# Two-layer hybrid trunk on one core: constants packed into two transfers, modulation weights in rotating slots, a lead of six staggered weight blocks

## The chip, the cores and the metric

The program runs on one core of one Trainium2 chip. A core has a matrix engine (TensorE, PE in the profile), a vector engine (VectorE, DVE), an activation engine (ScalarE, ACT), a general engine (GpSimd, POOL) and an engine that here only issues transfers (SyncE, SP). Every engine runs its own instructions in a fixed order and waits on semaphores for the others. The metric is the device time of one execution in microseconds (us), the lower the better.

## The reference

Two layers act on 256 context tokens and 256 latent tokens of 1024 features. Every sub-layer is RMSNorm, a shift and scale that a linear map makes from the conditioning vector, a body, and a gated residual add. The bodies are a SwiGLU with 2816 hidden features (half weight, twice per layer) and a mixer: in layer 0 eight attention heads beside 512 channels of an S5 state-space model, in layer 1 Hyena convolutions beside RG-LRU recurrences. Cut to what matters here:

```python
def adaln_params(cond, w, b):
    m = jax.nn.silu(cond) @ w + b
    return m.reshape(cond.shape[0], 1, N_MOD, D_MODEL)

def ffn_half_step(h, m, k, g, w_gate, w_up, w_down):
    shift, scale, gate = m[:, :, 3 * k], m[:, :, 3 * k + 1], m[:, :, 3 * k + 2]
    hn = modulate(rmsnorm(h, g), shift, scale)
    return h + 0.5 * gate * swiglu(hn, w_gate, w_up, w_down)
...
    for i in range(DEPTH):
        last = i == DEPTH - 1
        m_lat = adaln_params(c, mod_w[i], mod_b[i])
        m_ctx = adaln_params(c_ctx[None, :], mod_w[i], mod_b[i])
        ...
        lat = ffn_half_step(lat, m_lat, 0, norm_ffn1[i], *ffn1)
        cx = ffn_half_step(cx, m_ctx, 0, norm_ffn1[i], *ffn1)
        ...
            y_ctx, y_lat = even_mixer(h_ctx, h_lat, cos, sin, ...)
        lat = lat + m_lat[:, :, 5] * y_lat
        ...
    return rmsnorm(lat, final_norm)
```

## The kernel before

Features lie on the 128 partitions (eight feature tiles), the 512 tokens of both streams on the free axis. A float32 product is made as three matrix products of split parts (`mm3`, L145 to L151): high weight by high x (L149), high weight by low x (L150), low weight by high x (L151). `wload` (L136) loads a raw weight block of 128 x 1024 on SP's queue (L139), ACT casts its high part (L141), and DVE makes the low part (L142).

The Tile framework's scheduler sets the order of each engine's instructions from the order of the program, from priorities (`high_priority`) and from its own cost model; so an edit in one place can move instructions elsewhere. SP and ACT issues take eight completion semaphores in rotation, and an issue waits until the transfer that used its semaphore before has landed.

The work around the change is the lead, the first norm and the first products of the first half SwiGLU:

- `build` (L1233) loads the residual in four transfers (L1242), the condition `ct`, the S5 parameters (L463), the modulation weights of the first sub-layer `mw0` in eight tiles of two 512 KB halves (L1266), five constants behind tile 0 (L103: `sel`, `ident`, `modb`, `gain`, `sig`), and four weight blocks behind tiles 0 and 1. Eight smaller constants (`qkvn`, `rope`, `s5_d`, `s5_bg`, `lru_p`, `hy_cw`, `hy_b`, `lru_cw`) are loaded one by one where their stages begin in the program. Tile 5 of `mw0` sits in the `m` slots, tile 6 in the `sc` slot, the others in the `h` slots. The background modulation's condition `c2` (1 MB, L199) needs the `sc` slot too.
- `square_add` (L265, L269, L270) squares the residual on ACT and adds on DVE. `rstd_stats` sums over partitions on PE (L236) and finds 1/rms in three Newton steps on DVE (L241 to L249); `rstd_rows` spreads it over the partitions with the identity matrix (L256).
- `mod_first` (L172) makes shift and scale of one feature tile on PE: sixteen matmuls with `mw0` (L179), a copy on ACT (L188), four small matmuls with `sel` (L191), then bias and gain on DVE (`mod_fix`, L165, L168). Its PSUM tile comes from the pool `pm` (six buffers), which the products use too; the pool `ps` has two buffers.
- `norm_tile` (L278) gives a normalised tile: L287 on DVE, the high part on ACT (L292), the low part on DVE (L294). `norm_proj` (L297) with `lead` then makes, tile by tile, the products of the four blocks, twelve matmuls of 512 columns per tile.

Background work runs beside the SwiGLU: `mod_job` makes the later shifts, scales and gates on DVE (L215), and `s5_prepare` makes the S5 matrices (`s5_small` L455 first). In the even mixer, eight S5 passes (`s5_states`, `s5_out`) are interleaved with the products of the heads; a pass loads its matrices just ahead of its use (L920, L924) into the `x` slots. `lru_decay` (L1039) makes the constant `kap` of layer 1 from `lru_p`.

## Time and profile before

| what | us |
| --- | --- |
| median of three runs | 1826.03 |
| lowest and highest of them | 1825.6, 1826.72 |
| span of the profiled execution | 1825.2 |
| PE busy in the span | 1742.0 (95%) |
| DVE busy | 1307.9 (72%) |
| ACT busy | 684.6 (38%) |
| POOL busy | 37.0 (2%) |

The profile is one execution of the program. Its own time is given as its span, 1825.2 us, from the first to the last recorded work; the timed runs lie 0.4 to 1.5 us above it. Rows name an engine, a line of the kernel (L149), and the tiles written and read (out<-in). "Idle before" names what the engine waited for. PEclk is the clock that TensorE was granted, as a share of full speed.

### The profile page before, as it was taken

The page shows a single profiled execution, that of the slowest core. Times are in us where ns is not written, and L with a number is a line of the kernel's source. Part 1 is how long each engine was busy: PE and PEld are TensorE (multiplying, and loading weights), DVE is VectorE, ACT ScalarE, POOL GpSimd, SP SyncE. Part 2 cuts the span into 40 slices and gives each one's busy share as a digit, 9 for nine tenths or more (in the row PEclk, how much of TensorE's full clock was granted, in tenths as well). Part 3 has the DMA queues.
Part 4 walks back from the last instruction along what each step waited for, and adds up shares of the span by engine and source line. Part 5 has one row for each costly group of instructions (what it writes and reads, how often), then busy time and mean ns, then how long its engine had stood idle before and what let it go on. Part 6 is the DMA issues. An engine that isn't in the chain of part 4 may idle for free.

```text
span 1825.2 us, 24880 instructions
## 1 busy us (share of the span) xinstructions
PE 1742.0 (95%) x9364; PEld 1456.1 (80%) x9364; DVE 1307.9 (72%) x2582; ACT 684.6 (38%) x1082; POOL 37.0 (2%) x57
## 2 busy tenths in 40 slices
PE   5999999997999998999999999999999989789997
PEld 3778777787877787778888888888888888589997
DVE  7999999898578667775666677766653476975555
ACT  4433333333345654222222233222122247554442
POOL 0000000001000000000000010000000000010000
PEclk9999999998998999999999999999999999889998
DMA  8466666652465452664554533554533225236562
GB/s 320 167 213 203 207 205 202 211 193 96 124 187 160 131 170 89 191 208 141 159 184 150 161 116 124 175 174 152 171 116 93 81 81 198 71 130 194 181 190 92
DMA packets 108057, 292.64 MB, mean 160 GB/s; under 512 B 21217, under 2 KB 36449, under 8 KB 107681
## 3 DMA queue, kind: packets, MB, share of 16 engines
q1 hardware_dynamic: 102368, 287.39, 49.2%
q10 hardware_dynamic: 4928, 2.10, 0.6%
q0 software_dynamic: 640, 1.57, 0.3%
q8 instruction: 73, 1.20, 0.3%
q14 instruction: 48, 0.39, 0.1%
HBM read 272.20 MB, written 18.28 MB: 159 GB/s over the span
## 4 chain that ended last, share of the span: by engine, by line
PE 83%; DVE 9%; DMA 3%; ACT 2%; issue 1%; SPq 1%; DVEq 0%; ACTq 0%
PE mm L149 26%; PE mm L150 26%; PE mm L151 26%; DVE w L142 1%; DMA raw<-in_wgu_dram 1%; DVE acc L270 1%; DVE rs_y L249 1%; ACT w L141 1%; DMA x<-d_g 1%; DMA h<-in_modw_dram 1%; DMA x<-d_v 0%; SPq L943 0%; DVE rs_a L247 0%; DVE nt L287 0%; DVE junk L215 0%
## 5 line engine op out<-in xcount | busy, mean ns | idle before, releaser
L150 PE MATMUL mm<-x,w 128*128 128x512 f32 (+1 forms) x1792 | 631.6, 355 | 3.3 <-DVE x L294 3.3
L151 PE MATMUL mm<-x,w 128*128 128x512 f32 (+1 forms) x1792 | 630.1, 354 | 0.0
L149 PE MATMUL mm<-x,w 128*128 128x512 f32 (+1 forms) x1792 | 613.9, 357 | 11.4 <-ACT x L292 9.9
L141 ACT CAST w<-raw 128x1024 fp32r<-128x1024 f32 (+2 forms) x328 | 332.5, 1018 | 532.8 <-issue 267.4
L142 DVE TENSOR_TENSOR w<-raw,w 128x1024 fp32r<-128x1024 f32 (+2 forms) x318 | 376.5, 1187 | 164.0 <-ACT w L141 163.3
L149 PEld LDWEIGHTS mm<-x,w 128*128 128x128 f32 x1792 | 334.9, 192 | 65.8 <-ACT x L292 10.9
L150 PEld LDWEIGHTS mm<-x,w 128*128 128x128 f32 x1792 | 343.4, 192 | 52.2 <-DVE x L294 4.3
L151 PEld LDWEIGHTS mm<-x,w 128*128 128x128 f32 x1792 | 343.1, 192 | 49.3 <-issue 1.8
L215 DVE CUSTOM_DVE_ANT_0 junk<-m,sc 128x1024 f32<-128x1024 f32 x256 | 312.4, 1220 | 2.2
L149 PE MATMUL mm<-h,w 128*128 128x512 f32 (+1 forms) x776 | 270.3, 351 | 0.0
L150 PE MATMUL mm<-h,w 128*128 128x512 f32 (+1 forms) x776 | 270.1, 349 | 0.0
L151 PE MATMUL mm<-h,w 128*128 128x512 f32 (+1 forms) x776 | 269.8, 349 | 0.0
L150 PEld LDWEIGHTS mm<-h,w 128*128 128x128 f32 x776 | 146.2, 188 | 21.2 <-issue 1.4
L149 PEld LDWEIGHTS mm<-h,w 128*128 128x128 f32 x776 | 145.9, 189 | 21.5 <-issue 1.1
L151 PEld LDWEIGHTS mm<-h,w 128*128 128x128 f32 x776 | 146.2, 188 | 20.3 <-issue 0.4
L394 DVE SCALAR_TENSOR_TENSOR res<-mm,mraw,res 128x256 f32<-128x256 f32 x192 | 86.1, 479 | 97.1 <-PE mm L151 96.6
L422 DVE TENSOR_TENSOR h<-h,mm 128x512 f32<-128x512 f32 (+1 forms) x88 | 54.6, 620 | 125.2 <-PE mm L151 108.5
L421 ACT ACTIVATE h<-mm 128x512 f32<-128x512 f32 (+1 forms) x88 | 47.9, 544 | 238.3 <-PE mm L151 238.2
L292 ACT ACTIVATE x<-nt,mraw 128x256 fp32r<-128x256 f32 x88 | 43.0, 506 | 75.3 <-DVE nt L287 75.2
L156 DVE TENSOR_TENSOR h<-h,h 128x512 fp32r<-128x512 f32 (+1 forms) x88 | 54.4, 618 | 0.0
L155 ACT CAST h<-h 128x512 fp32r<-128x512 f32 (+1 forms) x88 | 49.6, 564 | 9.1 <-DVE h L422 9.0
L269 ACT ACTIVATE sq<-res 128x256 f32<-128x256 f32 x84 | 33.3, 413 | 50.4 <-DVE res L394 38.5
(324 smaller groups left out, 1437.1 us busy)
## 6 DMA issues: line engine op xcount, KB each, us to landing
raw<-in_wgu_dram SPq DMA_DIRECT2D x176, 512.0 KB, 3.6
m<-in_modw_dram SPq DMA_DIRECT2D x130, 512.0 KB, 4.2
raw<-in_wd_dram SPq DMA_DIRECT2D x64, 512.0 KB, 3.7
raw<-in_wd_dram SPq DMA_DIRECT2D x32, 384.0 KB, 3.3
raw<-in_od_in_dram SPq DMA_DIRECT2D x20, 512.0 KB, 3.5
h<-in_modw_dram SPq DMA_DIRECT2D x12, 512.0 KB, 10.4
raw<-in_ev_in_dram SPq DMA_DIRECT2D x10, 512.0 KB, 3.8
d_mb<-mbt SPq DMA_DIRECT2D x16, 256.0 KB, 3.0
```

Source lines behind the costliest of these rows:

```text
L141: nc.scalar.copy(w[:, 0, :n], raw[:, :n])
L142: (nc.gpsimd if pool else nc.vector).tensor_sub(w[:, 1, :n], raw[:, :n], w[:, 0, :n])
L149: mm(ps, lhsT=wh, rhs=xh, start=first and i == 0, stop=False)
L150: mm(ps, lhsT=wh, rhs=xl, start=False, stop=False)
L151: r = mm(ps, lhsT=wl, rhs=xh, start=False, stop=last and i == n - 1)
L155: self.nc.scalar.copy(hi, src)
L156: self.nc.vector.tensor_sub(lo, src, hi)
L215: nc.vector.tensor_tensor_reduce(self.junk, w, self.sc[:, v, :], 1.0, 0.0, ALU.mult, ALU.add, raw[:, dt, v : v + 1])
L292: self.last_act = nc.scalar.activation(x[:, 0, c0:c1], y, AF.Identity, bias=b)
L394: self.nc.vector.scalar_tensor_tensor(r, ps[:, c0:c1], gate[:, i, VEC[h] : VEC[h] + 1], r, op0=ALU.mult, op1=ALU.add)
L421: nc.scalar.activation(s[:, 0, lo:hi], pg[:, lo:hi], AF.Silu)
L422: nc.vector.tensor_mul(s[:, 1, lo:hi], s[:, 0, lo:hi], pu[:, lo:hi])
```

## The change

It does these things:

- Thirteen constants lie in one array `small` of 128 x 698 floats. `packed` loads its first 333 columns (`sel`, `ident`, `modb`, `gain`, `sig`; 170 KB) with one transfer on ACT's queue and the other 365 columns (187 KB; `rope` is padded from 64 to 128 partitions) with one transfer on POOL's queue, both ahead of all other work on these queues; `ct` moves to ACT's queue too. All later loads of single constants go.
- Every fourth `mw0` tile sits in the `m` slots, the others in the `h` slots in rotation. The `sc` slot stays free, so `c2` goes out on SP as soon as its turn comes: behind `mw0` tile 3, ahead of the lead blocks 4 and 5.
- `LEAD = (0, 0, 1, 2, 3, 4)`: six blocks instead of four are made in the lead. A block is loaded behind the `mw0` tile that its number names, and its products start with that feature tile, where it also makes up for the tiles before. Blocks 4 and 5 keep their two parts in `h` slots.
- `mod_first` takes its PSUM tile from `ps`, since six blocks fill `pm`.
- The first step of `s5_prepare` is emitted behind the loads and with a lower priority.

```diff
+SMALL = dict(sel=(2,), ident=(P,), modb=(2, 9, KT), gain=(7, KT), sig=(3,), qkvn=(5,), s5_d=(4,), s5_bg=(4,), lru_p=(2, 3, 4),
+             hy_cw=(12, 4), hy_b=(4,), lru_cw=(4, 5), rope=(NTOK,))
+LEAD = (0, 0, 1, 2, 3, 4)
...
+    def packed(self):
+        n = [math.prod(sh) for sh in SMALL.values()]
+        tl = self.const([P, sum(n)], "small")
...
+        cut = sum(n[:5])
+        self.nc.scalar.dma_start(tl[:, :cut], self.t["small"][:, :cut])
+        self.nc.gpsimd.dma_start(tl[:, cut:], self.t["small"][:, cut:])
...
+        if tag is None:
+            w = self.wp.tile([P, 2, 1024], F32R, tag="w", name=self.uid("w"))
+            hi, lo = w[:, 0], w[:, 1]
+        else:
+            hi, lo = (self.slot(tag, [P, 1024], F32R) for _ in range(2))
...
     def mod_first(self, i):
-        ps = self.pm()
+        ps = self.ps()
...
-                for w, ps in zip(ws, pss):
-                    self.mm3(ps, self.wparts(w, KT)[i : i + 1], self.parts(xs[i : i + 1], 0, T2), i == 0, i == KT - 1)
+                for w, ps, k0 in zip(ws, pss, LEAD):
+                    for j in range(0 if k0 == i else i, i + 1) if k0 <= i else ():
+                        self.mm3(ps, self.wparts(w, KT)[j : j + 1], self.parts(xs[j : j + 1], 0, T2), j == 0, j == KT - 1)
...
-        self.lp = self.const([P, 2, 3, 4], "lru_p", self.t["lru_p"])
+        self.lp = self.sml["lru_p"]
...
+        nc.scalar.dma_start(self.ct, t["ct"])
+        self.packed()
...
-            if i == 0:
-                nc.sync.dma_start(self.ct, t["ct"])
-                s5 = self.s5_prepare()
-                next(s5)
...
-            if i == 6:
-                w = self.slot("sc", [P, 2, 4, 2 * P])
-                self.mw0.append([w[:, r] for r in range(2)])
-            else:
-                self.mw0.append([self.slot("m" if i == 5 else "h", [P, 4, 2 * P]) for _ in range(2)])
+            self.mw0.append([self.slot("m" if i % 4 == 3 else "h", [P, 4, 2 * P]) for _ in range(2)])
             for r in range(2):
                 nc.sync.dma_start(self.mw0[i][r], t["modw0"][i, :, r])
-            if i == 0:
-                small()
-            if i < 2:
-                self.w0 += [self.wload(t["wgu"][0, i, g], D) for g in range(2)]
+            for b, k in enumerate(LEAD):
+                if k == i:
+                    self.w0.append(self.wload(t["wgu"][0, b // 2, b % 2], D, tag=None if b < 4 else "h"))
+        s5 = self.s5_prepare()
+        with self.tc.high_priority(offset=-400):
+            next(s5)
```

The scheduler then orders the engines anew. Three places matter here. The lines of the changed kernel are its own: its L296 is L269 of before, L206 is L179, L218 is L191, L263 is L236, L283 is L256, L176 is L149, L169 is L142, L314 is L287, L954 to L956 are L928 to L930.

First, ACT in the statistics (`sq` are squares of the residual). Before:

```order
L269 ACTIVATE sq_240<-res 128x256
L269 ACTIVATE sq_243<-res 128x256
L1247 ACT_TABLE_LOAD
L1247 ACTIVATE ct_127<-ct_127 128x256
L269 ACTIVATE sq_246<-res 128x256
L269 ACTIVATE sq_249<-res 128x256
```

Now:

```order
L296 ACTIVATE sq_246<-res 128x256
L296 ACTIVATE sq_249<-res 128x256
L1271 ACT_TABLE_LOAD
L1271 ACTIVATE ct_127<-ct_127 128x256
L1073 ACT_TABLE_LOAD
L1073 ACTIVATE kap_1078_7236<-kap_1078_7236 128x8
L296 ACTIVATE sq_252<-res 128x256
L296 ACTIVATE sq_255<-res 128x256
```

A second table load and the activation of `kap` now stand between the fourth square and the fifth. On DVE the operations of `kap` come to the front too, between the adds; the first of them, which reads `small`, stands ahead of the first add.

Second, PE from its first instruction to the first product (`mm` and `ps` are PSUM tiles, `ct` the condition). Before:

```order
L179 MATMUL mm_332<-h_175,ct_127 32x256 x4
L179 MATMUL mm_332<-h_176,ct_127 32x256 x4
L236 MATMUL ps_297<-inv_d,acc_236 128x1 x2
L236 MATMUL ps_297<-inv_d,acc_238 128x1 x2
L191 MATMUL mm_332<-sel,nt_341 128x2 x2
L179 MATMUL mm_347<-h_199,ct_127 32x256 x4
L179 MATMUL mm_347<-h_200,ct_127 32x256 x4
L191 MATMUL mm_347<-sel,nt_356 128x2 x2
L256 MATMUL ps_296<-ident,rs_y_303 128x128 x4
L149 MATMUL mm_292<-x_284,w_191 128x512
```

Now:

```order
L263 MATMUL ps_305<-inv_d,acc_242 128x1 x2
L206 MATMUL ps_340<-h_143,ct_127 32x256 x4
L263 MATMUL ps_305<-inv_d,acc_244 128x1 x2
L206 MATMUL ps_340<-h_144,ct_127 32x256 x4
L218 MATMUL ps_340<-small,nt_349 128x2 x2
L283 MATMUL ps_304<-small,rs_y_311 128x128
L206 MATMUL ps_355<-h_157,ct_127 32x256 x4
L206 MATMUL ps_355<-h_158,ct_127 32x256 x4
L283 MATMUL ps_304<-small,rs_y_311 128x128 x3
L218 MATMUL ps_355<-small,nt_364 128x2 x2
L206 MATMUL ps_385<-h_166,ct_127 32x256 x4
L206 MATMUL ps_385<-h_167,ct_127 32x256 x4
L176 MATMUL mm_298<-x_290,w_149 128x512
```

The statistics (L236, now L263) come ahead of and between the modulation matmuls, and a third modulation tile (ps_385) stands ahead of the first product; 355 and 385 need a buffer of `ps` that the tile before has left. On DVE, around the first normalised tile (`nt`), before:

```order
L249 SCALAR_TENSOR_TENSOR rs_y_303<-rs_a_304,rs_y_303 128x1 x4
L142 TENSOR_TENSOR w_205<-raw_203,w_205 128x1024
L447 TENSOR_TENSOR sb_20_163<-sb_20_163 128x64
L165 TENSOR_TENSOR mraw_0_282<-mm_347,modb 128x2
L165 TENSOR_TENSOR mraw_1_283<-mm_347,modb 128x2
L142 TENSOR_TENSOR w_210<-raw_208,w_210 128x1024
L446 TENSOR_SCALAR sb_20_163<-sb_20_163 128x64
L168 SCALAR_TENSOR_TENSOR mraw_1_283<-mraw_1_283,gain 128x2
L287 SCALAR_TENSOR_TENSOR nt_363<-res,mraw_1_283,ps_296 128x256
L287 SCALAR_TENSOR_TENSOR nt_366<-res,mraw_1_283,ps_296 128x256
```

Now:

```order
L274 SCALAR_TENSOR_TENSOR rs_a_312<-rs_y_311,rs_v_310 128x1 x4
L276 SCALAR_TENSOR_TENSOR rs_y_311<-rs_a_312,rs_y_311 128x1 x4
L169 TENSOR_TENSOR w_163<-raw_161,w_163 128x1024
L314 SCALAR_TENSOR_TENSOR nt_371<-res,mraw_1_289,ps_304 128x256
L314 SCALAR_TENSOR_TENSOR nt_374<-res,mraw_1_289,ps_304 128x256
L192 TENSOR_TENSOR mraw_0_288<-ps_355,small 128x2
L192 TENSOR_TENSOR mraw_1_289<-ps_355,small 128x2
L169 TENSOR_TENSOR w_172<-raw_170,w_172 128x1024
```

One weight split instead of two stands ahead of the first normalised tile, and the reads of the second modulation tile (ps_355) stand behind it. The S5 operations (`sb`) begin 71 rows into DVE's order; before they began with its sixth.

Third, PE in the even mixer, at the last two S5 passes (L928 to L930, now L954 to L956, twelve rows each; L843 and L849, now L869 and L875, transpose the heads' probabilities). Before:

```order
L930 MATMUL ps_5400<-hh_5249,x_5389 128x64
L849 MATMUL mm_5627<-ident,p_5537 128x128 x4
L843 MATMUL mm_5696<-ident,p_5587 128x128 x4
L928 MATMUL ps_5489<-x_4291,x_5480 128x64
L929 MATMUL ps_5489<-hh_5350,x_5478 128x64
```

Now:

```order
L955 MATMUL ps_5392<-hh_5241,x_5381 128x64
L956 MATMUL ps_5392<-hh_5241,x_5381 128x64
L954 MATMUL ps_5481<-x_4283,x_5472 128x64
L955 MATMUL ps_5481<-hh_5342,x_5470 128x64
L956 MATMUL ps_5481<-hh_5342,x_5470 128x64
```

The last two passes now follow one another directly. Earlier in the mixer the heads' products stand further ahead of the passes: between the second and the third pass there are now a score product and five value products (L810, L862 of before) more than there were.

## Rows read from the trace of the kernel before

**Rows 1.** The page's chain that ended last, its shares by engine.

```profile
PE 83%; DVE 9%; DMA 3%; ACT 2%; issue 1%; SPq 1%; DVEq 0%; ACTq 0%
```

**Rows 2.** Table by stretch; columns: stretch, busy time of each engine, PEclk, DMA share, GB/s.

```profile
14.00:18.00 4.00, 3.62 (x20) 2.72 (x20) 3.20 (x14) 2.22 (x3) 0.00 (x0) 1.00 0.81 263
18.00:29.00 11.00, 5.09 (x28) 3.04 (x28) 9.20 (x51) 3.61 (x6) 0.00 (x0) 1.00 1.02 402
65.00:420.00 355.00, 355.00 (x1698) 284.95 (x1697) 325.35 (x651) 126.61 (x200) 0.93 (x9) 1.00 0.63 202
```

**Rows 3.** Time line of SP's queue; columns: start, duration (us), engine, line, operation, tiles, count.

```profile
5.04 0.45 SPq L103 DMA_DIRECT2D sel<-in_sel_dram  x1
...
9.18 0.33 SPq L103 DMA_DIRECT2D sig<-in_sig_dram  x1
11.30 1.61 SPq L139 DMA_DIRECT2D raw<-in_wgu_dram  x2
```

**Rows 4.** Waits of SP's queue from 0 to 70: us in total, times, longest.

```profile
SPq L103 <- DMA h<-in_modw_dram: 2.1, 2, 1.1
```

**Rows 5.** DMA issues (0 to 50, then the even mixer): count, KB, median us to landing.

```profile
ident<-in_ident_dram SPq DMA_DIRECT2D x1, 64.0 KB, 8.7
...
d_y<-ys POOLq DMA_DIRECT2D x8, 128.0 KB, 2.8
```

**Rows 6.** Time line of ACT, 6 to 29 us; releaser of idle time in brackets.

```profile
6.40 1.28 ACT L1247 ACT_TABLE_LOAD   x1
...
10.39 3.31 ACT L269 ACTIVATE sq<-res 128x256 f32<-128x256 f32 x7 [0.16 <-DVE acc L270]
...
23.76 1.04 ACT L141 CAST w<-raw 128x1024 fp32r<-128x1024 f32 x1 [0.71 <-DMA raw<-in_wgu_dram]
...
28.06 0.91 ACT L292 ACTIVATE x<-nt,mraw 128x256 fp32r<-128x256 f32 x2 [1.98 <-DVE nt L287]
```

**Rows 7.** Time line of DVE, 13 to 28 us.

```profile
13.75 0.42 DVE L270 TENSOR_TENSOR acc<-acc,sq 128x256 f32<-128x256 f32 x1
...
16.80 0.16 DVE L241 TENSOR_SCALAR rs_v<-ps 128x4 f32<-128x4 f32 x1 [0.53 <-PE ps L236]
...
22.66 0.37 DVE L249 SCALAR_TENSOR_TENSOR rs_y<-rs_a,rs_y 128x1 f32<-128x1 f32 x4
24.83 1.23 DVE L142 TENSOR_TENSOR w<-raw,w 128x1024 fp32r<-128x1024 f32 x1 [1.80 <-ACT w L141]
...
27.55 0.87 DVE L287 SCALAR_TENSOR_TENSOR nt<-res,mraw,ps 128x256 f32<-128x256 f32 x2
```

**Rows 8.** Time line of PE, 12 to 41 us.

```profile
12.71 2.26 PE L179 MATMUL mm<-h,ct 128*32 128x256 f32 x16 [12.71 <-DMA h<-in_modw_dram]
...
23.98 2.05 PE L256 MATMUL ps<-ident,rs_y 128*128 128x128 f32 x8
29.02 2.08 PE L149 MATMUL mm<-x,w 128*128 128x512 f32 x4 [2.99 <-ACT x L292]
...
36.07 0.50 PE L191 MATMUL mm<-sel,nt 128*128 128x2 f32 x4
36.43 1.18 PE L149 MATMUL mm<-x,w 128*128 128x512 f32 x4
...
39.84 1.07 PE L179 MATMUL mm<-h,ct 128*32 128x256 f32 x16
40.73 1.05 PE L179 MATMUL mm<-m,ct 128*32 128x256 f32 x16
```

**Rows 9.** Time line of PE behind the lead blocks.

```profile
63.22 0.50 PE L149 MATMUL mm<-x,w 128*128 128x512 f32 x1 [0.69 <-ACT w L141]
...
64.16 0.51 PE L149 MATMUL mm<-x,w 128*128 128x512 f32 x1 [0.21 <-ACT w L141]
```

**Rows 10.** Time line of PE in the even mixer.

```profile
540.81 2.80 PE L810 MATMUL mm<-q,q 96*128 96x256 f32 x8
550.72 0.66 PE L928 MATMUL ps<-x,x 128*128 128x64 f32 x2 [7.11 <-DMA x<-d_v]
```

More of the change, by code (lines that the diff above doesn't have):

```diff
@@ L104, in const @@
         return tl
+    def packed(self):
+        n = [math.prod(sh) for sh in SMALL.values()]
+        tl = self.const([P, sum(n)], "small")
+        c0 = 0
+        self.sml = {}
+        for (nm, sh), k in zip(SMALL.items(), n):
+            a = tl[:, c0 : c0 + k]
+            names = "abc"[: len(sh)]
+            if len(sh) > 1:
+                a = a.rearrange(f"p ({' '.join(names)}) -> p {' '.join(names)}", **dict(zip(names, sh)))
+            self.sml[nm] = a
+            c0 += k
+        cut = sum(n[:5])
+        self.nc.scalar.dma_start(tl[:, :cut], self.t["small"][:, :cut])
+        self.nc.gpsimd.dma_start(tl[:, cut:], self.t["small"][:, cut:])
     def pm(self):
@@ L133, in need, with wload @@
         return self.mod[l, m]
-    def wload(self, src, n, pool=False):
+    def wload(self, src, n, pool=False, tag=None):
         nc = self.nc
@@ L139, in wload @@
         nc.sync.dma_start(raw[:, :n], src)
-        w = self.wp.tile([P, 2, 1024], F32R, tag="w", name=self.uid("w"))
-        nc.scalar.copy(w[:, 0, :n], raw[:, :n])
-        (nc.gpsimd if pool else nc.vector).tensor_sub(w[:, 1, :n], raw[:, :n], w[:, 0, :n])
-        return w
+        if tag is None:
[3 more added lines that the diff above has]
+            hi, lo = (self.slot(tag, [P, 1024], F32R) for _ in range(2))
+        nc.scalar.copy(hi[:, :n], raw[:, :n])
+        (nc.gpsimd if pool else nc.vector).tensor_sub(lo[:, :n], raw[:, :n], hi[:, :n])
+        return hi, lo
     def mm3(self, ps, w, x, first=True, last=True):
@@ L362, in wparts @@
     def wparts(self, w, n, m=P, o=0):
-        return [(w[:, 0, o + i * m : o + (i + 1) * m], w[:, 1, o + i * m : o + (i + 1) * m]) for i in range(n)]
+        return [(w[0][:, o + i * m : o + (i + 1) * m], w[1][:, o + i * m : o + (i + 1) * m]) for i in range(n)]
     def down(self, blocks, xs, gate, halves, last, n):
@@ L405, in ffn @@
         wgu = t["wgu"][idx]
-        blocks = [wgu[f, g] for f in range(2) for g in range(2)]
-        xs, pss = self.norm_proj(l, k, halves, blocks if lead else blocks[:3], lead)
+        blocks = [wgu[0, 0], wgu[0, 1], wgu[1, 0]]
+        xs, pss = self.norm_proj(l, k, halves, [None] * len(LEAD) if lead else blocks, lead)
         if lead is not None:
@@ L722, in values_in @@
                     xh, xl = (ckv[i][:, a, j * P : (j + 1) * P] for a in range(2))
-                    wh, wl = (wv[:, a, i * 512 : (i + 1) * 512] for a in range(2))
+                    wh, wl = (wv[a][:, i * 512 : (i + 1) * 512] for a in range(2))
                     nc.tensor.matmul(ps, lhsT=xh, rhs=wh, start=i == 0, stop=False)
@@ L1240, in build @@
         self.ct = self.slot("ct", [P, KT, 32])
+        nc.scalar.dma_start(self.ct, t["ct"])
+        self.packed()
+        for nm in ("sel", "ident", "modb", "gain", "sig"):
+            setattr(self, nm, self.sml[nm])
         for i in range(0, KT, 2):
             nc.sync.dma_start(self.res[:, i : i + 2, :], t["xt"][:, i : i + 2, :])
-            if i == 0:
-                nc.sync.dma_start(self.ct, t["ct"])
-                s5 = self.s5_prepare()
-                next(s5)
         nc.scalar.activation(self.ct, self.ct, AF.Silu)
@@ L1431, in _layout @@
     o["lru_w"] = wg.transpose(1, 0, 2, 3)
+    o["small"] = cat([o.pop(nm).reshape(P, -1) for nm in SMALL], axis=1)
     return {k: np.ascontiguousarray(v, dtype=np.float32) for k, v in o.items()}
```

18 lines of the change are left out of this document (5 added, 13 removed).

## The prediction

> **What bounds the kernel now.** I read the chain of waits first: 83% of the span is TensorE (PE) and 9% VectorE (DVE) [rows 1]. So the change can win only where PE stands idle or runs slowly, and can lose only by making PE wait. The table by stretch says where [rows 2]: from 65 to 420 us PE is busy the whole time, DVE 325.35 of 355 us, while from 0 to 29 us PE does next to nothing. Every edit of this change acts in the first 65 us or moves DVE work out of them, so the time lines of the first 35 us come next, engine by engine.
>
> They show one chain. The residual lands, ScalarE (ACT) squares it, the last seven squares end at 13.70 [rows 6], DVE's last add ends at 14.17, the first Newton step of 1/rms starts at 16.80 and the last ends at 23.03 [rows 7]. PE spreads the result over the partitions by 26.03 [rows 8], DVE then makes two weight splits of 1.23 each, from 24.83 on, and starts the first normalised tile at 27.55 [rows 7], ACT makes its high part until 28.97 [rows 6], and the first product starts at 29.02 [rows 8]. The first products run 0.52 us each (2.08 us for four), later ones one every 0.23 us. After the lead there are two short stalls on weight casts, 0.69 and 0.21 us [rows 9]; from 64.16 us on PE does not wait again until after 420 [rows 2].
>
> **Where before stands at the same work.** The change does six blocks of eight tiles in the lead, 6 x 8 x 3 = 144 products; before does 96 there and the other 48 after it. The first three of those 48 are through at 64.16 and the rest come 0.2315 us apart: 64.16 + 45 x 0.2315 = 74.6 us. I compare with this point, because behind it both programs have the same PE work.
>
> **The change, part by part.**
>
> *Constants in two transfers on ACT's and POOL's queues.* Before, SP issues five of them between 5.04 and 9.51, and the next weight block goes out only at 11.30 [rows 3], because each issue waits for an earlier transfer to land [rows 4] and these small transfers land late (the 64 KB one 8.7 us after its issue) [rows 5]. From 14 to 18 us the DMA engines then move 263 GB/s, against 402 in the next stretch [rows 2]; filling that gap is worth 4 x (402 - 263) / 402 = 1.4 us of earlier landing for what follows. On the path this is worth something only where a landing is the last wait; in the chain below it is not. I book 0. The bounds: a gain of 1.4, and a loss if the POOL transfer is late, since DVE's first op now reads it. POOL's transfers later in the kernel land 2.8 us after their issue [rows 5]; so 0 here too.
>
> The Trainium skill ("Trainium Kernel Development and Optimization", Key Constraints) says that DMAs issued from SP, ACT and POOL share the same 16 engines and that issuing from several only saves issue time. By it the landings would hardly move, and the fast rival below would not happen. The waits above show more than issue time being lost, so the trace does not bear the rule out fully, but it keeps that rival's chance under one third.
>
> *LRU constant (kap) moved to the front.* ACT gets a table load and a tiny activation between squares 4 and 5. Such a load takes 1.28 us [rows 6]; the activation I put at 0.2. If all of it is exposed, the squares end at 15.2 instead of 13.70: +1.5. If the last squares wait for the residual anyway it is 0. Seven squares in one run without a wait [rows 6] are nearest to the exposed end; I take +1.5. DVE's 25 kap operations take the places that S5 operations had between the adds, so nothing more.
>
> *First normalised tile.* The adds end at 15.7. PE has its modulation matmuls of tile 0 between the statistics, as before behind them, and the 1/rms chain (23.03 - 16.80 = 6.2 us) starts at 17.2 and ends at 23.4. The spreading matmuls (2.05 us, after a start that lagged 0.95) [rows 7, 8] end at about 26.0. Only one weight split, not two, now stands ahead of the first normalised tile, so it starts at 26.0 instead of 27.55.
>
> *Modulation tile 2 ahead of the first product, in a small PSUM pool.* The pool has two slots and 1/rms holds one, so each modulation tile waits until DVE has read the one before. PE's tile 2 comes before the first product and must wait for DVE's read of tile 1, behind the first normalised tile (0.87 us): it starts at 27.3 and takes about 2.2 (sixteen took 2.26 at 12.71) [rows 8]. First product: **29.5**, against 29.02. The earlier tile is lost again to this slot.
>
> *Lead of six blocks.* From there PE needs 144 x 0.2315 = 33.3; five more modulation tiles, each 0.89 (39.84 to 40.73) for the sixteen matmuls and 0.36 (36.07 to 36.43) for the four small ones [rows 8], 6.3; the slow first products as before, 4 x (0.52 - 0.23) and 0.7 for what follows them until the full rate, 1.9; and one exposed slot wait of about 1.0 (my estimate for a copy and a few small DVE operations). 29.5 + 33.3 + 6.3 + 1.9 + 1.0 = **72.0**. The same sum for before gives 29.02 + 33.3 + 7.5 (six tiles) + 1.9 + 0.9 (the two stalls) = 72.6, and its 74.6 holds 2.0 us of small gaps more, where a tile of x was not ready. With six blocks PE has half as many products again to do per tile, so I take gaps and stalls away: the gain is 74.6 - 72.0 = 2.6. If the gaps stay it is 0.6, and if the slot wait is hidden too it is 3.6.
>
> *S5 preparation later, second condition load earlier.* The S5 operations that DVE did beside the statistics (about 55, 0.13 us apart, 7 us) now follow; the kap operations, about 3 us, come out of the later part. So 4 us more DVE work must fit behind, and there are 355 - 325.35 = 29.65 us of slack there [rows 2]. Booked at 0; without that cover 4 us. The 1 MB load of the condition goes ahead of blocks 4 and 5: at 402 GB/s 2.6 us, hidden because these blocks are first used after two tiles, after 37.
>
> *From 420 on.* What PE gains in the lead must last to 420; between, PE is the bound and DVE is not. DVE's order at the end of this sub-layer differs by one pair of modulation reductions only. The even mixer's attention heads and S5 passes are interleaved differently, by the same operations: booked at 0, bounds below.
>
> Sum against the profiled span: 1825.2 - 2.6 = 1822.6. The median of the runs, 1826.03, is 0.83 above that span; forecast **1823.4**. A measurement of this kernel can tell about 0.2%, 3.65 us, from no change, so this counts as the same.
>
> **Rivals.**
> *Fast: the lead is fed much earlier.* If the squares wait for the residual anyway, the 1.5 us are not paid, and the chain ends near 21.9; then the third weight block decides (23.76 before [rows 6], 22.4 with the DMA gap filled, plus 1.04 and 1.23 for cast and split: 24.6). First product at 26.6, slot waits hidden: 2.9 + 1.0 more. 1823.4 - 3.9 = **1819.5**. For it: the low rate from 14 to 18 us. Against it: the table load and the page's rule.
> *No gain.* PE's lead is lost where DVE decides, at the end of the sub-layer: the S5 work that moved back (4 us) makes PE wait for DVE there. **1826.0**. The gaps that stay in the lead would end near there too. For it: DVE at 92% from 65 to 420. Against: 30 us of slack.
> *Slow: one more wait in the even mixer.* Before, PE stands 7.11 us at 543 to 550 because the matrices of the second S5 pass are loaded late [rows 10]: their buffers are free only when DVE and the heads get that far. In the new order heads run ahead of the passes and the last two passes stand back to back. If a second pass comes to wait like this one, the price is 7.1: 1823.4 + 7.1 = **1830.5**. It decides as soon as PE reaches a pass without 7 us of head work ahead of it. Against: PE work between passes 2 and 3 has grown, not shrunk.
>
> **Numbers.** Forecast 0.42, of which 0.10 falls beyond 3.65 us faster if part of the fast case holds; fast 0.28; no gain 0.15; slow 0.15. Faster by over 0.2%: 0.38; within: 0.32 + 0.15 = 0.47; slower: 0.15. The forecast's own range is 1820 to 1826 (table load hidden or not, one to three slot waits, gaps that stay). The range goes from 2 us below the fast case, 1817.5, to the slow case, 1830.5.
>
> **What would show it.** Right: the first product at 29 to 30 us, the six blocks done at about 72, no wait on casts after that, PE full until about 424, the 7.11 us wait of the second pass still alone. Squares ending before 14 us would say that the table load is hidden. A first DVE op later than 8 us would say that POOL's transfer is late. The forecast is wrong if the first product moves by over 2 us, if PE shows waits between 75 and 420, or if the mixer between 530 and 632 is longer or shorter by more than 3 us.

## The result and the profile after

| | before | after |
| --- | --- | --- |
| median of four runs each, us | 1826.38 | 1838.49 |
| lowest and highest | 1825.6, 1827.68 | 1836.37, 1842.46 |
| span of the profiled execution | 1825.2 | 1834.5 (that run: 1836.53) |
| first product starts | 29.02 | 30.60 |
| 144th product starts | 74.72 | 74.58 |
| fifth SwiGLU product on DVE | 98.91 | 97.89 |
| first SwiGLU product on DVE behind the first down projection | 157.25 | 168.08 |
| first normalised tile of the even mixer | 435.74 | 448.61 |

The change makes the kernel slower: ratio 1.0069, interval 1.0057 to 1.0080, some 12 us. The forecast was 1823.4 with a range up to 1830.5.

The last five rows of the table are the same work in both programs (the same operation of its kind, counted from the start; a product of PE is one matmul of 512 columns). They say where the time goes: 1.0 us ahead at 98, 10.8 behind at 168, 12.9 behind at 448. The profiled execution ends 9.3 behind, so 3.6 us come back later; it is one of the two lower of its four runs.

PE's waits from 65 to 420 us; before this list is empty. Columns: engine, line, what it waited for; us in total, times, longest.

```profile
PE ps L622 <- DVE et L663: 4.7, 1, 4.7
PE ps L642 <- DVE mraw L197: 1.6, 1, 1.6
PE mm L176 <- DVE res L422: 0.8, 1, 0.8
```

L622 is the transposes of an S5 pass's matrices (`mb`), here of the second pass, and L642 the product behind them. The table by stretch of the changed kernel, for two stretches of [rows 2] and for the ten microseconds around these waits:

```profile
14.00:18.00 4.00, 1.81 (x12) 1.13 (x12) 3.39 (x17) 3.72 (x7) 0.00 (x0) 1.00 1.03 422
65.00:420.00 355.00, 347.89 (x1606) 276.43 (x1605) 326.15 (x680) 127.89 (x198) 0.94 (x9) 0.99 0.61 195
140.00:150.00 10.00, 6.76 (x24) 4.96 (x25) 10.00 (x24) 0.58 (x1) 0.00 (x0) 0.54 0.62 184
```

PE lost 7.1 of its 355 us, all of it here. DVE is full for these ten, and PE's granted clock falls to 0.54. The same place on PE's time line:

```profile
135.53 0.60 PE L622 MATMUL ps<-small,mb 128*128 128x128 f32 x4
140.81 1.09 PE L622 MATMUL ps<-small,mb 128*128 128x128 f32 x4 [4.68 <-DVE et L663]
143.49 0.65 PE L642 MATMUL ps<-gs,bank 128*32 128x128 f32 x8 [1.59 <-DVE mraw L197]
144.98 0.80 PE L176 MATMUL mm<-h,w 128*128 128x512 f32 x1 [0.84 <-DVE res L422]
145.57 0.63 PE L177 MATMUL mm<-h,w 128*128 128x512 f32 x1
145.99 0.63 PE L178 MATMUL mm<-h,w 128*128 128x512 f32 x1
...
151.06 0.39 PE L178 MATMUL mm<-h,w 128*128 128x512 f32 x1
```

From 144.98 to 151.06 the products are about 0.43 apart (the 1.2 GHz level) and then 0.23 again: fourteen products in 6.1 us, 2.8 more than at 0.23. With the waits that is 9.9 of the 11.9 us lost between the two marks. And DVE beside it, which PE waits for:

```profile
138.83 1.22 DVE L242 CUSTOM_DVE_ANT_0 junk<-m,sc 128x1024 f32<-128x1024 f32 x1
139.97 0.69 DVE L618 TENSOR_TENSOR mb<-mb,tm 128x512 f32<-128x512 f32 x1
```

DVE makes `mb` in its turn, behind modulation sums of 1.22 us each. In PE's own order these transposes stand inside the first down projection, behind six of its eight feature tiles (108 of its 144 products). The six tiles fill the six buffers of `pm`; the product at 144.98 opens the seventh tile and needs a buffer that a residual add (`res`) has read. The adds wait for the gate, which the modulation sums make and L197 halves (L170 before). DVE after the change, then before:

```profile
143.26 0.17 DVE L197 TENSOR_SCALAR mraw<-mraw 128x16 f32<-128x16 f32 x1
...
144.05 4.39 DVE L422 SCALAR_TENSOR_TENSOR res<-mm,mraw,res 128x256 f32<-128x256 f32 x11
```

```profile
131.01 3.22 DVE L394 SCALAR_TENSOR_TENSOR res<-mm,mraw,res 128x256 f32<-128x256 f32 x8
```

Before, the adds start 6.1 us ahead of the end of PE's sixth tile (137.14); after the change they start 8.4 us behind it (135.69). By these rows DVE is 13 us later with its own work up to the gate, and PE would stand here until 144.05 even if the transposes stood elsewhere in PE's order.

The lead, on PE and DVE, to be read against [rows 7, 8]:

```profile
24.44 0.77 PE L283 MATMUL ps<-small,rs_y 128*128 128x128 f32 x2 [2.79 <-DVE rs_y L276]
25.13 1.94 PE L206 MATMUL ps<-h,ct 128*32 128x256 f32 x16
27.00 1.45 PE L283 MATMUL ps<-small,rs_y 128*128 128x128 f32 x6
...
29.60 1.07 PE L206 MATMUL ps<-h,ct 128*32 128x256 f32 x16 [0.81 <-PE ps L218]
30.60 1.20 PE L176 MATMUL mm<-x,w 128*128 128x512 f32 x4
```

```profile
8.18 0.17 DVE L1072 SCALAR_TENSOR_TENSOR kap<-small 128x8 f32<-128x8 f32 x1 [6.65 <-DMA small<-in_small_dram]
...
19.17 0.16 DVE L268 TENSOR_SCALAR rs_v<-ps 128x4 f32<-128x4 f32 x1 [1.61 <-PE ps L263]
...
28.49 0.87 DVE L314 SCALAR_TENSOR_TENSOR nt<-res,mraw,ps 128x256 f32<-128x256 f32 x2 [2.85 <-PE ps L283]
```

The spreading of 1/rms (L283) is cut in two by a modulation tile of 1.94 us, and the first normalised tile starts at 28.49.

### The profile page after: what moved, and what is told of

Same layout as the page of the kernel before. It is cut to its first block, busy times and chain, and to the rows that moved or that the text cites. A ratio compares the mean times of both kernels' runs of the same rounds, so it can differ in the third digit from the quotient of the medians.

```text
span 1834.5 us, 24867 instructions
## 1 busy us (share of the span) xinstructions
PE 1739.4 (95%) x9364; PEld 1454.8 (79%) x9364; DVE 1311.6 (71%) x2582; ACT 684.1 (37%) x1083; POOL 37.7 (2%) x58
## 4 chain that ended last, share of the span: by engine, by line
PE 86%; DVE 9%; DMA 2%; ACT 2%; issue 1%; SPq 1%; DVEq 0%; ACTq 0%
PE mm L176 27%; PE mm L177 26%; PE mm L178 26%; DVE w L169 1%; DVE acc L297 1%; DMA x<-d_g 1%; PE mm L836 1%; DVE rs_y L276 1%; DVE rs_a L274 1%; PE ps L283 1%; PE ps L206 1%; SPq L969 0%; PE mm L1134 0%; DVE junk L242 0%; PE ps L263 0%
## 5 line engine op out<-in xcount | busy, mean ns | idle before, releaser
L177 PE MATMUL mm<-x,w 128*128 128x512 f32 (+1 forms) x1776 | 622.6, 353 | 2.7 <-DVE x L321 2.7
L178 PE MATMUL mm<-x,w 128*128 128x512 f32 (+1 forms) x1776 | 621.8, 353 | 0.0
L176 PE MATMUL mm<-x,w 128*128 128x512 f32 (+1 forms) x1776 | 604.5, 355 | 8.7 <-ACT x L319 7.0
L169 DVE TENSOR_TENSOR w<-raw,w 128x1024 fp32r<-128x1024 f32 (+2 forms) x316 | 373.6, 1185 | 161.1 <-ACT w L168 160.5
L177 PEld LDWEIGHTS mm<-x,w 128*128 128x128 f32 x1776 | 338.8, 191 | 51.0 <-DVE x L321 3.6
L176 PEld LDWEIGHTS mm<-x,w 128*128 128x128 f32 x1776 | 329.8, 191 | 62.2 <-ACT x L319 7.7
L178 PEld LDWEIGHTS mm<-x,w 128*128 128x128 f32 x1776 | 338.5, 191 | 48.5 <-issue 1.4
L176 PE MATMUL mm<-h,w 128*128 128x512 f32 (+1 forms) x776 | 271.1, 352 | 0.8 <-DVE res L422 0.8
L176 PEld LDWEIGHTS mm<-h,w 128*128 128x128 f32 x776 | 146.2, 189 | 22.8 <-DVE res L422 1.3
L422 DVE SCALAR_TENSOR_TENSOR res<-mm,mraw,res 128x256 f32<-128x256 f32 x192 | 85.7, 479 | 98.3 <-PE mm L178 97.6
L296 ACT ACTIVATE sq<-res 128x256 f32<-128x256 f32 x84 | 33.3, 413 | 52.3 <-DVE res L422 41.0
```

What stands on the lines that cost most here:

```text
L169: (nc.gpsimd if pool else nc.vector).tensor_sub(lo[:, :n], raw[:, :n], hi[:, :n])
L176: mm(ps, lhsT=wh, rhs=xh, start=first and i == 0, stop=False)
L177: mm(ps, lhsT=wh, rhs=xl, start=False, stop=False)
L178: r = mm(ps, lhsT=wl, rhs=xh, start=False, stop=last and i == n - 1)
L422: self.nc.vector.scalar_tensor_tensor(r, ps[:, c0:c1], gate[:, i, VEC[h] : VEC[h] + 1], r, op0=ALU.mult, op1=ALU.add)
```

## The experiments

The theory after this reading: **S5 work on the bound.** DVE, not only PE, sets the pace of the first half SwiGLU; the S5 operations that left DVE's idle time ahead of 29 us (DVE is busy 20.19 of 29 us before, 15.41 after) make PE wait at the S5 transposes. Rivals: **the early chain** (`kap` and the small PSUM pool delay the first product, and the rest follows from that); **the transposes' place** (DVE has room, only PE meets them too early); **six blocks** cost by themselves. The expectations number such theories as they came up in their batch. Each batch of runs had its own runs of before, with medians 1827.02 (first four), 1825.42 (next four), 1825.36 (four) and 1827.71 (last three); ratios are against these. The expected times often missed: (a) fell between its two theories, (b), (d), (h) and (q) came out 2 to 10 us above every range named, and both runs of (t) 2 to 6 us below.

| run | first product | DVE behind first down projection | first tile, even mixer | median | ratio, interval |
| --- | --- | --- | --- | --- | --- |
| before | 29.02 | 157.25 | 435.74 | 1826.38 | 1 |
| after | 30.60 | 168.08 | 448.61 | 1838.49 | 1.0069 (1.0057 to 1.0080) |
| a_s5_early | 33.31 | 166.28 | 444.25 | 1831.18 | 1.0034 (1.0020 to 1.0048) |
| b_s5_late | 28.73 | 180.35 | 459.38 | 1849.31 | 1.0121 (1.0101 to 1.0141) |
| c_kap_late | 29.48 | 168.40 | 447.19 | 1839.52 | 1.0074 (1.0059 to 1.0089) |
| d_lead4 | 31.43 | 177.82 | 456.74 | 1848.40 | 1.0125 (1.0110 to 1.0140) |
| e_s5_early_kap_late | 30.98 | 162.81 | 440.78 | 1830.96 | 1.0037 (1.0025 to 1.0048) |
| f_delay10 | 31.62 | 157.11 | 445.89 | 1835.85 | 1.0058 (1.0043 to 1.0073) |
| f_delay10c | 29.38 | 154.38 | 444.22 | 1832.80 | 1.0041 (1.0026 to 1.0056) |
| h_lead6_only | 31.62 | 162.18 | 440.83 | 1837.45 | 1.0063 (1.0047 to 1.0079) |
| g_relief_before | 28.36 | 158.58 | 429.36 | 1819.84 | 0.9964 (0.9951 to 0.9977) |
| g_relief_after | 31.69 | 159.33 | 431.52 | 1823.28 | 0.9989 (0.9979 to 0.9999) |
| g_relief_lead6 | 32.84 | 163.98 | 434.89 | 1824.83 | 0.9992 (0.9983 to 1.0002) |
| p_packed_lead4 | 27.15 | 158.52 | 437.21 | 1826.54 | 1.0005 (0.9996 to 1.0014) |
| q_ps_only | 31.45 | 163.37 | 442.23 | 1834.15 | 1.0036 (1.0023 to 1.0050) |
| t_nopool | 28.56 | 156.96 | 431.47 | 1815.14 | 0.9936 (0.9923 to 0.9949) |
| t_nopool_packed | 26.86 | 157.48 | 434.18 | 1818.57 | 0.9956 (0.9943 to 0.9970) |

**S5 early again, in the changed kernel (a), and S5 late alone, in the kernel before (b).**

The diff is (a)'s, on after; (b) moves the same lines the other way, on before.

```diff
+            if i == 0:
+                s5 = self.s5_prepare()
+                next(s5)
...
-        s5 = self.s5_prepare()
-        with self.tc.high_priority(offset=-400):
-            next(s5)
```

> The changed kernel with one part undone: the first step of the S5 preparation is emitted where it was before, behind the first residual load, without the lower priority. Theory 1 (the S5 operations that DVE did in idle time before 29 us now come later; DVE is about 5 us behind when PE reaches the S5 transposes at the first down projection, PE stands 7.1 us there and runs some 3 us at the lower clock behind it): the three waits between 135 and 145 us are under 1 us together, no stretch at the lower clock there, and the time is 1824 to 1828 us. Theory 2 (the six lead blocks and the new order of loads shift DVE's work, wherever the S5 step stands): the waits stay at 5 us or more, the time stays at 1835 to 1839.

> The kernel before with that one part alone: the first S5 step behind the loads with the lower priority. Theory 1: PE, which waited nowhere between 65 and 420 us, waits 5 to 10 us for DVE in the S5 transposes of the first half SwiGLU, and the time is 1833 to 1839. Theory 2: no such wait above 1 us, 1825 to 1828.

In (a) the waits at the S5 transposes nearly go. PE's list for 65 to 420 us:

```profile
PE mm L178 <- DVE w L169: 1.1, 1, 1.1
PE ps L218 <- ACT nt L215: 0.5, 1, 0.5
PE ps L622 <- DVE mraw L192: 0.5, 1, 0.5
```

The ratio falls from 1.0069 to 1.0034: half the loss, 6 us. The other half stays, and begins earlier: S5 and `kap` now share DVE ahead of 1/rms, and the first product starts at 33.31. (The profiled execution of (a) is 5 us above its median, so its marks after 100 us are on the high side.)

In (b), one part of the change alone costs more than the whole of it, 22 us, with the first product no later than before (28.73). PE waits for DVE at the same work (L594 and L614 are L622 and L642 of the changed kernel), 15 us in these three rows:

```profile
146.42 1.09 PE L594 MATMUL ps<-ident,mb 128*128 128x128 f32 x4 [9.31 <-DVE mb L590]
150.53 1.09 PE L594 MATMUL ps<-ident,mb 128*128 128x128 f32 x4 [3.02 <-DVE mb L590]
154.24 0.66 PE L614 MATMUL ps<-gs,bank 128*32 128x128 f32 x8 [2.62 <-DVE mraw L165]
```

So the early chain is not needed for this loss, and the S5 work moved back is enough for it.

**`kap` late again (c), and four blocks in the lead (d), both in the changed kernel.**

```diff
...
-        self.lp = self.sml["lru_p"]
+        self.lp = self.const([P, 2, 3, 4], "lru_p", self.t["lru_p"])
```

```diff
-LEAD = (0, 0, 1, 2, 3, 4)
+LEAD = (0, 0, 1, 1)
```

> The changed kernel with lru_p taken out of the packed array and loaded alone where it was, so that the kap operations and their table load leave the start. Theory 1: squares end 1.5 to 2.5 us earlier (before 14 us) and the first product comes at 28 to 29; the S5 wait stays, as long or up to 3 us longer, so the time is 1834 to 1839. A third theory (the kap operations are what pushes DVE behind): the waits between 135 and 145 us shrink by 3 us or more and the time falls under 1833.

> The changed kernel with four lead blocks, placed as before (0, 0, 1, 1), everything else as changed. Theory 1: the S5 waits of PE between 130 and 150 us stay at 5 us or more and the time is 1835 to 1840. Theory 2: they fall under 1 us, and the time is 1825 to 1830.

(c): the first normalised tile is 2.0 us earlier (26.50) and the first product 1.1, but the total is the same as the change's. What the lead gains is lost at the same place in the first down projection, where PE waits for DVE. So `kap` costs nothing in the sum here. (d) is 10 us slower than the change: here six blocks are worth 10 us. Six of them are there at the 144th product already, 80.58 against 74.58: six blocks give PE half as many products again per normalised tile. That these cover more of the time in which the next tile is not ready is argued, not shown.

The place is the same in all four kernels with this loss. The first residual add starts behind the end of PE's sixth tile by 8.4 us in the change, 19.6 in (b), 11.1 in (c) and 13.7 in (d); in the other thirteen kernels of the table it starts 3.7 to 17.6 us ahead of it.

**Both (e), and the S5 work behind the first step later (f).**

(e) is (a) and (c) together. The diff is that of (f_delay10), on after; (f_delay10c) is the same on (c). It starts the rest of the S5 work, behind its first step, ten steps later.

```diff
+        def later(gen, n):
+            for _ in range(n):
+                yield
+            yield from gen
-        self.start(s5, 2.5)
+        self.start(later(s5, 10), 2.5)
```

> The changed kernel with the S5 step early (as in a_s5_early) and lru_p loaded alone. In a_s5_early the first product came at 33.3 us and the lead was 10 us late, because S5 and kap operations both stood between the adds and the Newton steps on DVE. Theory: without the 25 kap operations and the table load the first product comes at 29 to 31 us, the lead gains 3 to 8 us against a_s5_early, and the time is 1824 to 1829. Rival (it is the six blocks' own weight splits that delay the tiles of x on DVE): the first product comes earlier, but the lead ends no more than 2 us earlier and the time stays at 1829 to 1833.

> The changed kernel with ten empty steps ahead of the background S5 job, which moves the transposes of S5 pass 1 from right ahead of the first down projection (after product 396 on PE) to after product 523. Theory 1a (the loss is where PE meets these transposes; DVE catches up behind it in its slack): no PE wait between 65 and 415 us above 1 us, no half clock there, the first down projection at the time of before or 1 us earlier, time 1824 to 1829 us. Theory 1b (DVE is the bound of the whole sub-layer, the wait only shows there): the missing 5 to 10 us come back as waits later, at the latest as a longer DVE stretch at 418 to 450, time 1833 to 1839.

> The same delay, and lru_p loaded alone where it was, so that no kap operation stands at the start. Theory 1a: the lead is about 0.4 to 1 us earlier than with the delay alone, time 1823 to 1829. Theory 1b: 1833 to 1841.

(e) ends where (a) does, 1.0037; some 5.5 us are left with neither S5 nor `kap` to blame. (f_delay10) tells the place from the amount. In PE's order the transposes of the first S5 pass move from products 237 and 274 to 322 and 355, those of the second from 396 to 523 and 559. DVE's work for them moves too, so the first residual add comes at 127.13, and the mark behind the down projection is back to 157.11, as before the change. But the first tile of the even mixer is 10 us late all the same. Its table by stretch and PE's time line at the end of the sub-layer:

```profile
160.00:420.00 260.00, 260.00 (x1260) 208.81 (x1259) 238.72 (x478) 93.35 (x149) 0.67 (x6) 1.00 0.66 205
420.00:450.00 30.00, 13.52 (x92) 11.45 (x91) 28.81 (x77) 10.94 (x21) 5.05 (x4) 0.66 0.33 110
```

```profile
430.98 1.09 PE L622 MATMUL ps<-small,mb 128*128 128x128 f32 x4 [5.01 <-DVE mb L618]
...
436.88 1.09 PE L622 MATMUL ps<-small,mb 128*128 128x128 f32 x4 [4.81 <-DVE et L659]
...
440.59 0.66 PE L642 MATMUL ps<-gs,bank 128*32 128x128 f32 x8 [2.63 <-DVE mraw L192]
```

The same kind of waits, 12.5 us, return at the end, where DVE is busy 28.81 of 30 us and PE 13.52. (Before, PE waits 8.2 us there for 1/rms, and here 1.9.) The place of the S5 work decides where the debt is paid, not whether: the ratio 1.0058 lies inside the interval of the change. An edit that moves the transposes in PE's order alone was not run. (f_delay10c), without `kap` at the start as well, has its first product 2.2 us earlier and a median 3 us lower; the two intervals overlap, so whether `kap` costs something here stays open.

**Six blocks, rotating slots and the small PSUM pool alone (h), on before.**

```diff
+LEAD = (0, 0, 1, 2, 3, 4)
...
-        ps = self.pm()
+        ps = self.ps()
...
+            for b, k in enumerate(LEAD):
+                if k == i:
+                    self.w0.append(self.wload(t["wgu"][0, b // 2, b % 2], D, tag=None if b < 4 else "h"))
```

> The kernel before with the six staggered blocks alone (with the rotating slots of the modulation weights and the small PSUM pool, which they need); constants and S5 step as before. Forecast's view (six blocks fill PE's gaps in the lead): the same work is done 1 to 3 us earlier at 75 us, time 1823 to 1826. Rival (DVE, which makes S5 operations, weight splits and tiles of x in the same time, is the bound of the lead): PE waits for tiles of x or modulation, the lead ends 3 to 8 us later than before's at the same work, time 1828 to 1834.

With S5 early and the constants as before this part still costs 1.0063, and its first product is at 31.62. So the second half of the loss sits in here.

**Less DVE work (g).** Of each modulation sum of layer 0 that runs beside the first half SwiGLU only the first 512 of 1024 features are summed, in before, in after and in (h); the output is made from these half sums.

```diff
+                n = 512 if l == 0 and m < 8 else D
...
-                            self.junk, w, self.sc[:, v, :], 1.0, 0.0, ALU.mult, ALU.add, raw[:, dt, v : v + 1]
+                            self.junk[:, :n], w[:, :n], self.sc[:, v, :n], 1.0, 0.0, ALU.mult, ALU.add, raw[:, dt, v : v + 1]
```

> The kernel before, with half of one kind of DVE work left out: the 96 modulation reductions that run beside the first half SwiGLU read 512 of their 1024 columns, so that the later shifts, scales and gates of layer 0 are made from half of the features. That takes about 96 x 0.55 = 50 us off DVE up to 430 us. Theory 1b (DVE is the bound of that sub-layer): the long DVE stretch at 418 to 443 us shrinks and PE waits there for under 4 us instead of 7.7, time 1816 to 1821 us. Theory 1a (PE is the bound there): no more than 3 us are gained, 1823 to 1826.

> The changed kernel with the same DVE work left out. Theory 1b: with DVE in slack the S5 transposes no longer hold PE up, the waits at the first down projection go, and the changed kernel loses at most 3 us to the relieved kernel before, or gains up to 2 (the forecast's 2.6 us of the lead show): 1814 to 1823. Rival (the loss has a cause that DVE's load has no part in, such as the order of loads or the clock): it stays 8 to 12 us above the relieved kernel before, 1826 to 1833.

> The kernel before with the six blocks alone and the same DVE work left out. Six blocks alone cost 12 us with DVE loaded. Theory 1b: relieved, they cost under 3 us against the relieved kernel before: 1815 to 1823. Rival (their loss is made in the lead, before the modulation reductions start, by tiles of x and by the small PSUM pool): the lead stays late by 3 to 6 us at the same work and the time is 1822 to 1828.

The changed kernel with this relief, 65 to 420 us:

```profile
65.00:420.00 355.00, 355.00 (x1691) 283.63 (x1690) 294.34 (x731) 134.65 (x211) 0.97 (x9) 1.00 0.64 205
```

PE is full again and has no wait in this stretch; the first residual add is 3.7 us ahead of PE. Against the equally relieved kernel before, the change costs 3.4 us (1823.28 less 1819.84) instead of 12, and (h) 5.0 instead of 12. What stays in (h) is there at the 144th product already (79.30 against 74.74), as the rival in its expectation says: that part is made in the lead. Before itself gains 5.5 us, although PE waits for nothing between 65 and 420 in it: DVE's lateness there shows only at the end, where PE waits 8.2 us for 1/rms without the relief and 2.4 with it.

**The constants alone (p), the PSUM pool alone (q).**

(p) is (e) with four blocks and the large pool, so that of the change the packed constants and the slots are left. (q) is one line on before.

```diff
-LEAD = (0, 0, 1, 2, 3, 4)
+LEAD = (0, 0, 1, 1)
...
-        ps = self.ps()
+        ps = self.pm()
```

```diff
     def mod_first(self, i):
-        ps = self.pm()
+        ps = self.ps()
```

> The packed constants with the early condition load and rotating slots, but without what hurt: lru_p loaded alone and late, the S5 step early, four lead blocks, modulation tiles in the large PSUM pool. If taking the small transfers off SP's queue helps at all, the first product comes 1 to 2 us earlier than 29.02 and the time is 1822 to 1825.5; if it is hidden, as the forecast booked, it is within 1 us of the kernel before; if DVE's order is upset again, over 1828.

> The kernel before with one edit: the modulation tiles of the lead take their PSUM tile from the small pool, as in the changed kernel. PE's order then has modulation tile 2 ahead of the first product, as there. If the pool's single free slot is what makes the lead late: the first product comes at 31 to 32 us instead of 29.02 and the fifth pair of blocks 2 to 5 us later than in the kernel before, time 1828 to 1832. If it is the six blocks: first product within 1 us of 29.02, time 1825 to 1827.

(p) starts its first product 1.9 us earlier than before and takes the same time, 1.0005. (q), one line, costs 1.0036, 6.4 us, and shows the first product at 31.45. Its PE time line:

```profile
23.70 0.77 PE L256 MATMUL ps<-ident,rs_y 128*128 128x128 f32 x2 [4.36 <-issue]
24.39 1.94 PE L179 MATMUL ps<-h,ct 128*32 128x256 f32 x16
26.26 1.65 PE L256 MATMUL ps<-ident,rs_y 128*128 128x128 f32 x6
...
29.60 1.93 PE L179 MATMUL ps<-h,ct 128*32 128x256 f32 x16 [1.04 <-issue]
```

It is the order of the changed kernel: a modulation tile inside the spreading of 1/rms, and the next one ahead of the first product. The loss is complete at the 144th product, which starts at 81.28 against 74.72. As (e), which has six blocks and the packed constants besides, ends at 1.0037, six blocks are worth about nothing where S5 is early; (h), with the constants as before, is even 1.0063. These comparisons run across batches.

**A version that beats both (t).** In the rows of before at the end of the first half SwiGLU, POOL's weight splits stand out. POOL, then DVE, of before:

```profile
421.65 2.38 POOL L142 TENSOR_TENSOR w<-raw,w 128x1024 fp32r<-128x1024 f32 x1 [14.75 <-ACT w L141]
424.93 2.45 POOL L142 TENSOR_TENSOR w<-raw,w 128x1024 fp32r<-128x1024 f32 x1 [0.89 <-ACT w L141]
```

```profile
421.71 2.41 DVE L635 TENSOR_TENSOR et<-et,sb 128x64 f32<-128x64 f32 x1
...
425.06 2.34 DVE L243 TENSOR_SCALAR rs_v<-rs_v 128x2 f32<-128x2 f32 x1
```

A DVE operation of two columns takes 2.34 us while POOL works. So the ten splits go to DVE:

```diff
-        ws = [self.wload(s, D, i > 0) for i, s in enumerate(srcs)]
+        ws = [self.wload(s, D) for i, s in enumerate(srcs)]
```

> The kernel before with the ten weight splits that POOL makes ahead of the norms given to DVE. Before, the two at 421.65 and 424.93 us took 2.4 us each and a small DVE operation beside each took 2.4 instead of 0.2 us. If POOL's split holds DVE up and DVE is the bound there: DVE pays 2 x 1.22 us and saves 2 x 2.2, the first normalised tile of the even mixer comes 1 to 3 us earlier than 435.74, time 1821 to 1825. If DVE is not the bound, or the stretch has another cause: within 1 us of before, or 1 to 3 us slower.

> The same edit on p_packed_lead4 (packed constants, four blocks, S5 step early, kap late), the version of the change that was not slower. If both hold: 1821 to 1825 us; if packing is worth nothing, the same as t_nopool.

DVE at the same work in (t_nopool):

```profile
421.31 1.22 DVE L142 TENSOR_TENSOR w<-raw,w 128x1024 fp32r<-128x1024 f32 x1 [0.16 <-ACT w L141]
...
422.96 0.21 DVE L635 TENSOR_TENSOR et<-et,sb 128x64 f32<-128x64 f32 x1
...
424.11 0.17 DVE L243 TENSOR_SCALAR rs_v<-rs_v 128x2 f32<-128x2 f32 x1
```

Ratio 0.9936, 12.6 us faster than before and some 24 faster than the change by the ratios. The traced execution, the slowest of its five, is 7.9 us shorter than that of before; 4.3 of these are there at the first tile of the even mixer. With the packed constants (t_nopool_packed) it is 1818.57: faster than before too, but no faster than without them.

## Why the prediction was wrong

The forecast was 15 us too low, and outside its range. Its steps in turn:

- **What bounds the kernel.** This is where it failed first. The 83% of PE in [rows 1] and its full 355 us [rows 2] were read as "between, PE is the bound and DVE is not". (g_relief_before) shows otherwise: less DVE work in that stretch gives 5.5 us with the same products on PE (the S5 transposes among them move, as from 345 and 385 to 306 and 334).
- **S5 preparation later, "booked at 0; without that cover 4 us".** The failed step of the sum. It set 4 us of work against 355 - 325.35 = 29.65 us of slack. DVE's waits in that stretch are for PE's products (7.7 us at L422, 3.6 at L394), for ACT's casts (7.1) and for S5 tables that land (4.1): pauses of at most 1.9 us, at places that DVE's order fixes. Work that came later did not fit into them: after the change DVE still stood idle 28.85 us of that stretch, and yet its first residual add came 8.4 us too late for PE. The room to count was the 6.1 us by which that add is ahead of PE's sixth tile before, and the delay to set against it was 13 us and not 4: 4.8 us more idle time of DVE ahead of 29 us, 2.4 us for two more weight splits ahead of the add, and some 6 us that are not traced to single operations. The measured price is 7.1 us of waits and 2.8 at half clock in the change, 22 us in (b), 6 us by (a).
- **Modulation tile 2 in the small pool, first product 29.5.** Measured 30.60, a miss of 1.1 us that is small by luck. The slot was seen to hold tile 2 back. What was overlooked stands in the prediction's own rows of PE's order: tile 1 (ps_355) between the first spreading matmul and the other three, 1.94 us on the path to the first normalised tile, which came at 28.49 and not at 26.0 (the other 0.5 us is a later start of the spreading). Tile 2 itself then took 1.07 us and not 2.2, which gave half of the error back. The price of the pool alone is 6.4 us by (q), most of it after the first product.
- **Lead of six blocks, 72.0 against 74.6, a gain of 2.6.** Start of the 144th product: 74.58 against 74.72. The gain is 0.1, and 1.0 at the fifth SwiGLU product.
- **`kap`, +1.5.** The squares end at 16.0, 2.3 later than before. The table load was exposed, as taken (1.28 and 0.21 us), with 0.80 us more of waiting for DVE's adds:

```profile
8.63 1.28 ACT L1073 ACT_TABLE_LOAD   x1
...
11.54 4.46 ACT L296 ACTIVATE sq<-res 128x256 f32<-128x256 f32 x10 [0.80 <-DVE acc L297]
```

  Right for the lead, but it moves nothing at the end, by (c) and by (e) against (a).
- **Constants, 0.** Right by (p): 1.0005. The low DMA rate between 14 and 18 us did fill, 422 GB/s against 263. In (p) the modulation tile 1, in two halves, is used at 17.05 and 18.31, against 20.26 and 21.53 before, 3.2 us sooner: SP issues it at 7.14 instead of 13.86 us, with the constants and their waits [rows 3, 4] gone from its queue. The Trainium skill ("Trainium Kernel Development and Optimization", Key Constraints) says that issuing from several engines only saves issue time. For the landings the trace shows more than that: the issues of the five constants took 2.4 us on SP's queue, and the issue of tile 1 came 6.7 us sooner. POOL's transfer took 6.9 us, not 2.8, and DVE's first operation started at 8.18, later than the 8 us named as the sign of that; by (c), in which that operation is gone from the front, nothing in the total followed.

```profile
small<-in_small_dram POOLq DMA_DIRECT2D x1, 182.5 KB, 6.9
```

- **From 420 on, even mixer, 0.** About right: the change enters the mixer 12 to 13 us behind and leaves it about 12 behind, and the slow rival did not come. The long wait for the second pass's matrices is still alone:

```profile
562.08 0.66 PE L954 MATMUL ps<-x,x 128*128 128x64 f32 x2 [6.51 <-DMA x<-d_v]
```

- **The no-gain rival** had the mechanism, S5 work moved back that makes PE wait for DVE, but put it at the end of the sub-layer and at 2.6 us. It came inside the first down projection, at 10. Waits of PE between 75 and 420, which the prediction named as a sign against its forecast, are what the profile shows.

The whole, by the ratios: with six blocks in the kernel S5 late is worth 6 of the 12 us (1.0069 against 1.0034 in (a)), and the 6 that stay are what the PSUM pool costs alone (1.0036 in (q)). (By the medians of its batch (a) is 4.2 us above before.) The parts do not simply add: S5 late alone costs 22 us (b), and (d), which has the pool besides, 21. The pool was not taken out of the changed kernel by itself, as six blocks fill `pm`. By place it is otherwise: the change is not behind at its 144th product, for its six blocks cover the pool's gaps and DVE has not yet done the S5 work; it pays at the gate. (e) and (h) do the S5 work early and are 6 to 7 us behind at the fifth SwiGLU product already (105.08 and 105.68 against 98.91). DVE's work has to be done on one side or the other. What stays open is why (h) takes about 5 us more than (q) by the ratios: its traced execution, the fastest of its four, does not show them, for it enters the even mixer 5.1 us behind before, and (q) 6.5. Open is also why 3.6 us of the change's loss come back behind the first tile of the even mixer.

## What to carry to other kernels

- Idle time of an engine inside a stretch is not room for more work if it is made of short waits in a fixed order. Test it by taking work away from the engine that seems to have slack: if the kernel gets faster, that engine is on the path.
- Work done in an idle stretch at the start is free; before it is moved, look for the first place where the busy engine needs the other one's results, and by how much they are ahead there. Here the gate was 6 us ahead of PE before and 8 us behind after, and PE stood for 7 us and then ran at half clock for 6.
- A PSUM pool with one free slot turns an order into a chain. Count who holds its slots at the time.

## What the runs showed of the hardware

While POOL makes one of its ten weight splits, one DVE operation beside it stands nearly as long. All ten in before, min/median/max in ns:

```profile
L142 POOL TENSOR_TENSOR w<-raw,w x10: 2359/2384/2446, 421.7 to 1612.4; 128x1024 fp32r<-128x1024 f32 x10
```

Beside nine of these ten a DVE operation takes 2.2 to 2.5 us (beside the tenth 1.92) that takes 0.14 to 0.41 at its fastest, and eight of the nine belong to the sums and the Newton steps of 1/rms on the path between two sub-layers. The same split takes DVE 1.22 us. The Trainium skill ("SBUF — State Buffer", Who interferes with whom) says that a DVE instruction with two SBUF inputs contends with a GpSimd instruction that reads SBUF, that one in a mode with two ports contends with GpSimd, and that the lock is exclusive: whichever issues first holds the shared ports for its whole instruction. The rows agree with it: eight of the nine stretched operations read two or more tiles, and the ninth is a `TENSOR_SCALAR`, which that page names among those that can take both ports. With the splits on DVE the stretched operations at 421 and 425 us are gone and the kernel is 12.6 us faster; that this is the whole cause of the 12.6 was not tried. The split itself is also shorter on DVE, 1.22 against 2.38 us, and no run tells the two apart.
